# One 512-column matmul over both parts of the activations, with the halves added at eviction

## The chip, the core and the metric

One core of a Trainium2 chip runs the whole program as one launch. The metric is device time in microseconds. The kernel before takes 2003.37 us (median of 3 runs, 2002.3 to 2007.34). All times below are of one profiled execution of it, unless a run is named.

## The reference, cut to what matters

The input is 256 tokens of width 1024. A first block (gated linear attention, spatial gating, and product-key retrieval of experts) is followed by a second block (feed-forward, bidirectional retention with a Fourier branch, feed-forward). Nearly all the arithmetic is products of a 1024-wide activation with a weight. Four of them matter here:

```python
h = jnp.einsum('tkd,td->tk', u, xx)           # experts: scores with all 16384 rows of peer_u
a = (jax.nn.gelu(h) * gg)
u = h @ w_in                                  # second block: q, k, v, g, f, ga, gf
(jax.nn.sigmoid(ga) * r + jax.nn.sigmoid(gf) * fo) @ w_out
(jax.nn.silu(a) * b) @ w2                     # feed-forward, a and b from h @ w13
```

`einsum` over chosen experts is computed as a dense product with all 128 blocks of 128 experts, weighted by a matrix G that is zero where an expert was not chosen.

## The kernel before, in words

Activations stand transposed: 128 partitions, 8 chunks of the width (KD), 256 tokens (T). A unit of weights is a tile of 128 x 1024 float32, 512 KB, loaded by the SP queue into `raw` (three buffers). To keep accuracy with the float32r matmul, each weight is split into a rounded part `whi` and a rest `wlo`: ScalarE casts `raw` to `whi` (L108), VectorE subtracts to get `wlo` (L109). Both have three buffers, so the split of unit n+3 may begin when the matmuls of unit n are over. The activations are split likewise into `hi` and `lo` (`nhi`/`nlo`, `nxh`/`nxl`).

A product is three matmuls for each chunk (`mm3`, L245 to L247): `whi` with `hi`, `whi` with `lo`, `wlo` with `hi`; 24 of them make a unit. They accumulate in one half of a PSUM bank of 512 columns. `fm` (L392) is a unit whose result a function evicts.

`Emit.run` writes the instructions of all engines in program order, and each engine runs its own list in that order. After the matmuls of unit n it issues the split of unit n+3 (`fetch`), and then (`settle`) what was put off with `em.later`: the eviction of unit n. So on ScalarE and on VectorE the split of unit n+3 stands ahead of the eviction of unit n.

The stages that the change touches:

- Expert scores (`expert_u`, L1252): 128 units; ScalarE evicts with Gelu into `act` (two buffers, L1256), and POOL stores it to `uD`. In blocks 64 to 122 the matrix G is built in between: `gbuild` makes 32 sets of four float16 operations on VectorE (L1231 to L1234), and two groups of eight float16 matmuls for each set (L1243, L1244), evicted by ScalarE (L1248). A set is issued two units ahead of the first of its groups.
- Gates `sga` and `sgf` (`ev_gate`, L1667): 16 units, evicted with Tanh. In the same stretch VectorE and ScalarE normalize the context (`ctx`, `y`, L326 to L333) and make decay tables (`dk`, `dw`, `D`).
- Gate of retention (`gunit`, L1754): 16 units, evicted with Silu.
- Second feed-forward (`ffn`, `ctx is None`): its columns 8 to 21, two units each.

Names in the profile: `acc` and `wk` are PSUM banks, `scr` is scratch.

Of the kernel before, what the change touches and what calls it, by code (L numbers as in the profile page):

```python
# [11 lines left out]
F32 = mybir.dt.float32  # L12
F32R = mybir.dt.float32r
F16 = mybir.dt.float16
U16 = mybir.dt.uint16
AF = mybir.ActivationFunctionType
ALU = mybir.AluOpType
# [3 lines left out]
P = 128  # L21
T = 256
D = 1024
KD = D // P
# [10 lines left out]
TKE, GB0, GB1 = 63, 64, 58  # L35
# [102 lines left out]
class Halves:  # L138
# [5 lines left out]
    def __getitem__(self, key):  # L144
        p, d, t = key
        if isinstance(d, slice):
            n = d.start // 4
            return self.t[n][p, d.start - 4 * n:d.stop - 4 * n, t]
        return self.t[d // 4][p, d % 4, t]


def merge(main, fill, first=0, every=1.0):
# [46 lines left out]
def body(ctx, tc, I, out):  # L199
    nc = tc.nc  # L200
    act, dve, pe, pool = nc.scalar, nc.vector, nc.tensor, nc.gpsimd
# [8 lines left out]
    em = Emit(nc, rawp, splp, RAW, 3)  # L210
# [154 lines left out]
    def npair(pl, tag, width=T):  # L365

        full = T + 2 if pl is npool else T
        hi = pl.tile([P, KD, full], F32R, name=tag + "hi", tag=tag + "hi")
        lo = pl.tile([P, KD, full], F32R, name=tag + "lo", tag=tag + "lo")
        return hi[:, :, :width], lo[:, :, :width]  # L370

    def apair():
        return [npool.tile([P, T], F32R, name=n, tag=n, bufs=2) for n in ("ah", "al")]
# [10 lines left out]
    def chunks(o, hi, lo, x, width, order=range(KD)):  # L384

        xh, xl = x
        for k in order:
            sl = slice(k * P, k * P + P)
            mm3(o, hi[:, sl], lo[:, sl], xh[:, k, :width], xl[:, k, :width], k == order[0], k == order[-1])


    def fm(ap, x, evac, bank=bankB):  # L392

        def fn(hi, lo):
            ps = bank()
            chunks(ps[:, :T], hi, lo, x(), T)
            em.later(lambda: evac(ps))
        return ("w", ap, fn)
# [60 lines left out]
    def ffn(w13, w2, y, nx, wk, done, rest, early, ctx=None, mc=None):  # L459

        acc = Acc()
        hold = {}
        items = []

        def gate_c(j):
            ps = hold.pop(("c", j))
            s = wk().tile([P, T], F32, name="cs", tag="cs", bufs=1)  # L470
            act.activation(out=s, in_=ps[:, 0:T], func=AF.Silu)
            dve.tensor_tensor(out=s, in0=s, in1=ps[:, T:], op=ALU.mult)
            em.later(lambda: split(s, *mc(j)))

        def gate(j):
            pa_, pb_ = hold.pop(("ps", j, 0)), hold.pop(("ps", j, 1))
            both = ctx is not None and j >= early
            if j < early:
                s, silu, prod = gate_y(pa_, pb_, wk())
            else:  # L480
                w = 2 * T if both else T
                f = wk().tile([P, w], F32, name="s2", tag="s2", bufs=2)
                s = f[:, :T]

                def silu():
                    act.activation(out=f, in_=pa_[:, :w], func=AF.Silu)

                def prod():
                    dve.tensor_tensor(out=f, in0=f, in1=pb_[:, :w], op=ALU.mult)

            def low():
                hold["m", j] = apair()
                split(s, *hold["m", j])
                if both:
                    split(f[:, T:], *mc(j))

            if j < 2:
                silu()
                if ctx is not None:
                    prod()  # L500
                else:
                    em.later(prod, 1)
                em.later(low, 0 if ctx is not None else 1)
                return

            hold["low", j] = low
            if ctx is not None or j == NFF - 1:
                silu()
                prod()
            else:  # L510
                em.later(silu)
                em.later(prod, 1)

        def bank(j, half):
            if ctx is None:
                return bankA() if j == 2 else bankB()
            return bankA() if j == half == 1 else bankB()

        def up0(sp):
            if ctx is not None:  # L520
                c = hold["c", 0] = bankB()
                for n, (hi, lo) in enumerate(sp):
                    chunks(c[:, n * T:n * T + T], hi, lo, ctx(), T)
            ps = [bank(0, n) for n in range(2)]
            hold["ps", 0, 0], hold["ps", 0, 1] = ps
            mm3s([p[:, :T + 2] for p in ps], sp, *y(), T + 2)
            if ctx is not None:
                em.later(lambda: gate_c(0))

        def up(j, half):  # L530
            def fn(hi, lo):
                ps = hold["ps", j, half] = bank(j, half)
                if j >= early:
                    w = T if ctx is None else 2 * T
                    chunks(ps[:, :w], hi, lo, nx(), w)
                else:
                    if ctx is not None:
                        if half == 1:
                            hold["c", j] = bankA()
                        chunks(hold["c", j][:, half * T:half * T + T], hi, lo, ctx(), T)  # L540
                    chunks(ps[:, :T + 2], hi, lo, y(), T + 2)
                if half == 0:
                    if j < early and ctx is not None:
                        em.later(lambda: gate_c(j))
                    em.later(lambda: gate(j))
            return fn

        def down(j):
            def fn(hi, lo):
                mh, ml = hold.pop(("m", j))  # L550
                acc.step(hi, lo, mh, ml, j == 0, j == NFF - 1)
                f = hold.pop(("low", j + 2), None)
                if f is not None and ctx is None and j + 2 == NFF - 1:
                    em.soon.append(f)
                elif f is not None:
                    em.later(f, 0 if ctx is not None else 1)
                if j == NFF - 1:
                    done(acc)
            return fn

        def begun():
            rest()
            em.later(lambda: gate(0), 0 if ctx is not None else 1)

        items += [("w", [w13[0], w13[NFF]], up0), ("e", None, begun)]
        for j in range(1, NFF):
            items.append(("w", w13[NFF + j], up(j, 1)))
            items.append(("w", w13[j], up(j, 0)))
            if ctx is not None and j > 1:
                items.append(("w", w2[j - 2], down(j - 2)))  # L570
            elif 2 < j < NFF - 1:
                for n in (0, 1) if j == 3 else (j - 2,):
                    items.append(("w", w2[n], down(n)))

        for n in range(NFF - 2 if ctx is not None else NFF - 3, NFF):
            items.append(("w", w2[n], down(n)))
        return items
# [109 lines left out]
    sga = pa.tile([P, KD, T], F32, name="sga")  # L687
# [327 lines left out]
    items = []  # L1015
# [236 lines left out]
    def expert_u(b):  # L1252

        def ev(ps):
            u = B["pu"].tile([P, T], F32, name="act", tag="act", bufs=2)
            act.activation(out=u, in_=ps[:, :T], func=AF.Gelu_apprx_tanh)  # L1256
            pool.dma_start(out=uD[:, b, :], in_=u)  # L1257

        return fm(I["pu"][b], X2, ev)


    def first_q(ns):
# [32 lines left out]
    for j in range(NQ, 16):  # L1295
        n = min(j - 1, sc + (3 if j > NQ else 0))
# [98 lines left out]
    E_ = {}  # L1395
# [132 lines left out]
    def rest_f2():  # L1528
        def f():
            E_["r"] = root(ones_sum(E_["q"][:1], bankA))  # L1530
            table(AF.Silu)
            dve.reciprocal(out=E_["r"], in_=E_["r"])

        def norm():
            E_["nx"] = [E_["fp"].tile([P, KD, T], F32R, name=n) for n in ("nxh", "nxl")]
            late_norm(E_["x"], E_["r"], E_["g"], NX, lambda d: E_["h1"][:, d, :],
                      range(KD), modx[:, 48:56])
        em.later(f)
        em.later(norm, 5)
# [127 lines left out]
    def ev_gate(name, j):  # L1667

        def f(ps):
            act.activation(out=M[name][:, j, :], in_=ps[:, :T], func=AF.Tanh, scale=0.5)  # L1670
        return f


# [79 lines left out]

    def gunit(h, j):  # L1754
        def ev(ps):
            act.activation(out=E_["h1"][:, 4 * (h % 2) + j, :], in_=ps[:, :T], func=AF.Silu)
            if j == 3:
                table(AF.Sqrt)
        return fm(I["wg"][4 * h + j], XN, ev)

    def att_s(h):
        def f():
# [208 lines left out]
    i = [n for n, it in enumerate(f1) if it[0] == "w"][-NFF - 2]  # L1971
    f1[i:i] = [("e", None, lambda: x_gain("norm_mix_2", 24, 16, 0.5))]
    items += f1 + [("e", None, open_k)]
    items += [fm(I["wga"][j], XN, ev_gate("sga", j), bankA if j < 4 else bankB) for j in range(8)]
    items += [fm(I["wgf"][j], XN, ev_gate("sgf", j), bankB if j < 6 else bankA) for j in range(8)]
    items.append(("e", None, open_f))
    for g in range(2):
        items += tm(I["wf"][4 * g:4 * g + 4], [XN], ev_f(g), bankB if g else bankA)
# [121 lines left out]
```

## Time and profile before

| | us |
|---|---|
| median of 3 runs | 2003.37 |
| the profiled execution | 2002.91 |
| its span | 2001.2 |
| TensorE (PE) busy | 1986.2 |
| VectorE (DVE) busy | 1397.1 |
| ScalarE (ACT) busy | 1017.0 |
| POOL busy | 153.3 |

The span goes from the first to the last instruction. A busy PE overlaps its matmuls, so the time of one is read from start to start and not from its duration. The granted clock is at full speed in all 40 slices of the page.

### The profile page before, as it was taken

The page shows a single profiled execution, that of the slowest core. Times are in us where ns is not written, and L with a number is a line of the kernel's source. Part 1 is how long each engine was busy: PE and PEld are TensorE (multiplying, and loading weights), DVE is VectorE, ACT ScalarE, POOL GpSimd, SP SyncE. Part 2 cuts the span into 40 slices and gives each one's busy share as a digit, 9 for nine tenths or more (in the row PEclk, how much of TensorE's full clock was granted, in tenths as well). Part 3 has the DMA queues.
Part 4 walks back from the last instruction along what each step waited for, and adds up shares of the span by engine and source line. Part 5 has one row for each costly group of instructions (what it writes and reads, how often), then busy time and mean ns, then how long its engine had stood idle before and what let it go on. Part 6 is the DMA issues. An engine that isn't in the chain of part 4 may idle for free.

```text
span 2001.2 us, 37792 instructions
## 1 busy us (share of the span) xinstructions
PE 1986.2 (99%) x15348; PEld 1906.4 (95%) x15348; DVE 1397.1 (70%) x2282; ACT 1017.0 (51%) x1510; POOL 153.3 (8%) x296
## 2 busy tenths in 40 slices
PE   9999999999999999999999999999999999999998
PEld 8899999999999999999998888899989999999998
DVE  7668788977776666798876776588654556478555
ACT  6555545456766444545563333245644445446444
POOL 0000011111112101111000000010000000000000
PEclk9999999999999999999999999999999999999999
DMA  7656576766667777887664666677633334455653
GB/s 241 195 160 200 169 225 217 242 211 198 195 192 236 234 235 248 286 291 254 208 220 150 197 193 216 200 242 261 189 125 96 107 107 132 144 176 173 190 184 122
DMA packets 110094, 393.18 MB, mean 196 GB/s; under 512 B 14103, under 2 KB 14487, under 8 KB 109536
## 3 DMA queue, kind: packets, MB, share of 16 engines
q1 hardware_dynamic: 85968, 310.55, 48.5%
q0 software_dynamic: 22944, 77.52, 11.7%
q8 instruction: 120, 1.97, 0.4%
q10 hardware_dynamic: 1008, 2.70, 0.4%
q14 instruction: 54, 0.44, 0.1%
HBM read 371.84 MB, written 18.87 MB: 195 GB/s over the span
## 4 chain that ended last, share of the span: by engine, by line
PE 97%; DVE 1%; DMA 1%; ACT 1%; issue 0%; DVEq 0%; ACTq 0%; POOLq 0%
PE wk L245 18%; PE wk L247 18%; PE wk L246 18%; PE acc L246 10%; PE acc L247 10%; PE acc L245 10%; PE acc L416 2%; PE acc L417 2%; PE acc L418 2%; PE acc L1243 1%; PE acc L1244 1%; DMA raw<-w_dram 0%; PE acc L1080 0%; PE wk L259 0%; DVE wlo L109 0%; PE wk L1898 0%
## 5 line engine op out<-in xcount | busy, mean ns | idle before, releaser
L109 DVE TENSOR_TENSOR wlo<-raw,whi 128x1024 fp32r<-128x1024 f32 x587 | 717.0, 1223 | 494.8 <-ACT whi L108 490.5
L108 ACT CAST whi<-raw 128x1024 fp32r<-128x1024 f32 x587 | 614.8, 1048 | 682.0 <-PE wk L246 323.7
L245 PE MATMUL wk<-nhi,whi 128*128 128x256 f32 (+1 forms) x1744 | 496.9, 285 | 0.0
L247 PE MATMUL wk<-nhi,wlo 128*128 128x256 f32 (+1 forms) x1744 | 491.5, 282 | 0.3 <-DVE wlo L109 0.3
L246 PE MATMUL wk<-nlo,whi 128*128 128x256 f32 (+1 forms) x1744 | 489.7, 281 | 0.0
L246 PE MATMUL acc<-al,whi 128*128 128x256 f32 x1376 | 387.8, 282 | 0.1
L247 PE MATMUL acc<-ah,wlo 128*128 128x256 f32 x1376 | 387.7, 282 | 0.0
L245 PE MATMUL acc<-ah,whi 128*128 128x256 f32 x1376 | 387.7, 282 | 0.0
L246 PEld LDWEIGHTS wk<-nlo,whi 128*128 128x128 f32 x1744 | 329.6, 189 | 0.6 <-issue 0.5
L247 PEld LDWEIGHTS wk<-nhi,wlo 128*128 128x128 f32 x1744 | 329.4, 189 | 0.5 <-DVE wlo L109 0.5
L245 PEld LDWEIGHTS wk<-nhi,whi 128*128 128x128 f32 x1744 | 328.6, 188 | 0.9 <-issue 0.5
L246 PEld LDWEIGHTS acc<-al,whi 128*128 128x128 f32 x1376 | 259.2, 188 | 1.3 <-DVE al L377 0.5
L245 PEld LDWEIGHTS acc<-ah,whi 128*128 128x128 f32 x1376 | 259.2, 188 | 0.9
L247 PEld LDWEIGHTS acc<-ah,wlo 128*128 128x128 f32 x1376 | 259.3, 188 | 0.0
L246 PE MATMUL wk<-nxl,whi 128*128 128x512 f32 (+1 forms) x544 | 188.5, 346 | 0.0
L245 PE MATMUL wk<-nxh,whi 128*128 128x512 f32 (+1 forms) x544 | 188.2, 346 | 0.0
L247 PE MATMUL wk<-nxh,wlo 128*128 128x512 f32 (+1 forms) x544 | 187.4, 344 | 0.0
L376 ACT CAST ah<-early 128x256 fp32r<-128x256 f32 x128 | 52.1, 407 | 170.0 <-PE acc L247 165.2
L247 PEld LDWEIGHTS wk<-nxh,wlo 128*128 128x128 f32 x544 | 102.2, 188 | 13.2
L245 PEld LDWEIGHTS wk<-nxh,whi 128*128 128x128 f32 x544 | 102.1, 188 | 13.0
L246 PEld LDWEIGHTS wk<-nxl,whi 128*128 128x128 f32 x544 | 102.1, 188 | 11.8
L1257 POOL DMA_DIRECT2D uD<-act x128 | 69.3, 542 | 382.1 <-ACT act L1256 319.8
(534 smaller groups left out, 3210.9 us busy)
## 6 DMA issues: line engine op xcount, KB each, us to landing
raw<-pu_dram SPq DMA_DIRECT2D x128, 512.0 KB, 3.8
raw<-pv_dram SPq DMA_DIRECT2D x128, 512.0 KB, 4.3
row<-ada_dram POOLq DMA_DIRECT2D x59, 512.0 KB, 4.5
raw<-f13a_dram SPq DMA_DIRECT2D x44, 512.0 KB, 3.5
raw<-f2a_dram SPq DMA_DIRECT2D x44, 512.0 KB, 4.5
raw<-f13b_dram SPq DMA_DIRECT2D x44, 512.0 KB, 3.5
raw<-w_dram SPq DMA_DIRECT2D x41, 512.0 KB, 4.0
uD<-act POOLq DMA_DIRECT2D x128, 128.0 KB, 3.9
```

The costliest lines, as they stand in the source:

```text
L108: nc.scalar.copy(hi, r)
L109: nc.vector.tensor_tensor(out=lo, in0=r, in1=hi, op=ALU.subtract)
L245: pe.matmul(o, whi, xhi, start=start, stop=False)
L246: pe.matmul(o, whi, xlo, start=False, stop=False)
L247: pe.matmul(o, wlo, xhi, start=False, stop=stop)
L376: act.copy(hi, src)
L416: pe.matmul(o, xh[:, k, ts], hi[:, sl], start=k == 0, stop=False)
L417: pe.matmul(o, xh[:, k, ts], lo[:, sl], start=False, stop=False)
L418: pe.matmul(o, xl[:, k, ts], hi[:, sl], start=False, stop=k == KD - 1)
L1243: pe.matmul(o, p2[:, k, :, t], ph[:, k, :, t], start=True, stop=False)
L1244: pe.matmul(o, p2[:, k, :, t], p1[:, k, :, t], start=False, stop=True)
L1257: pool.dma_start(out=uD[:, b, :], in_=u)
```

## The change

For 125 units (expert blocks 63 to 127, the 16 gates, the 16 retention gates, and 28 of the second feed-forward) `hi` and `lo` of the activations stand side by side in one tile. `whi` meets both in one matmul of 512 columns, and `wlo` meets `hi` in one of 256: 16 matmuls for a unit and not 24. The bank then holds two halves. `fold` adds them: ScalarE copies the second half out of PSUM, VectorE adds the first half to it, and only then ScalarE applies Gelu, Tanh or Silu. Where no 512-column form is used, the two views `hi` and `lo` are read as before.

```diff
+    def wide(ps, hi, lo, x):
+        for k in range(KD):
+            sl = slice(k * P, k * P + P)
+            first = lambda: pe.matmul(ps.rearrange("p (a t) -> p a t", a=2), hi[:, sl], x.both[:, k], start=k == 0,
+                                      stop=k == KD - 1)
+            if k < KD - 1:
+                first()
+            pe.matmul(ps[:, :T], lo[:, sl], x[0][:, k, :], start=False, stop=False)
+            if k == KD - 1:
+                first()
+    def fold(out, ps):
+        act.copy(out, ps[:, T:])
+        dve.tensor_tensor(out=out, in0=ps[:, :T], in1=out, op=ALU.add)
...
-        return hi[:, :, :width], lo[:, :, :width]
+        return Pair(pl.tile([P, KD, 2, full], F32R, name=tag, tag=tag)[:, :, :, :width])
...
-                    act.activation(out=f, in_=pa_[:, :w], func=AF.Silu)
+                        act.activation(out=f, in_=f, func=AF.Silu)
...
+                        u = E_["p"].tile([P, T], F32, name="nn", tag="nn", bufs=3)
+                        fold(u, pb_)
+                        dve.tensor_tensor(out=f, in0=f, in1=u, op=ALU.mult)
+                if not both:
+                    fold(f, pa_)
...
-            act.activation(out=u, in_=ps[:, :T], func=AF.Gelu_apprx_tanh)
+            if b < TKE:
+                act.activation(out=u, in_=ps[:, :T], func=AF.Gelu_apprx_tanh)
+            else:
+                fold(u, ps)
+                act.activation(out=u, in_=u, func=AF.Gelu_apprx_tanh)
...
-            act.activation(out=M[name][:, j, :], in_=ps[:, :T], func=AF.Tanh, scale=0.5)
+            o = M[name][:, j, :]
+            fold(o, ps)
+            act.activation(out=o, in_=o, func=AF.Tanh, scale=0.5)
...
-            act.activation(out=E_["h1"][:, 4 * (h % 2) + j, :], in_=ps[:, :T], func=AF.Silu)
+            o = E_["h1"][:, 4 * (h % 2) + j, :]
+            fold(o, ps)
+            act.activation(out=o, in_=o, func=AF.Silu)
```

ScalarE's list in the expert stage while G is built, two units of the program before; what stands in brackets names the engines or queues whose semaphore is waited for (PE, DVE, DMAHW and DMASW for transfers).

```order
L108 CAST whi<-raw 128x1024 [waits DMAHW3_49,DVE_49,PE_49]
L1248 ACTIVATE G<-acc 128x4x128
L1256 ACTIVATE act<-wk 128x256 [waits DMASW6_49,PE_49,Activation_49]
L108 CAST whi<-raw 128x1024 [waits DMAHW4_49,DVE_49,PE_49]
L1248 ACTIVATE G<-acc 128x4x128
L1256 ACTIVATE act<-wk 128x256 [waits DMASW7_49,PE_49,Activation_49]
```

The same place of the changed program:

```order
L108 CAST whi<-raw 128x1024 [waits DMAHW3_49,PE_49]
L1293 ACTIVATE G<-acc 128x4x128
L412 COPY act<-wk 128x256 [waits DMASW6_49,Activation_49]
L1305 ACTIVATE act<-act 128x256 [waits DVE_49]
L108 CAST whi<-raw 128x1024 [waits DMAHW4_49,PE_49]
L1293 ACTIVATE G<-acc 128x4x128
L412 COPY act<-wk 128x256 [waits DMASW7_49,Activation_49]
L1305 ACTIVATE act<-act 128x256 [waits DVE_49]
```

One instruction for each unit is new on ScalarE, and the Gelu now waits for VectorE, with the next `whi` behind it.

VectorE's list at that place before (`p`, `ph` are the four operations of a set):

```order
L109 TENSOR_TENSOR wlo<-raw,whi 128x1024 [waits DMAHW1_49,PE_49,Activation_49]
L1231 TENSOR_TENSOR p_5511<-iota,i1T 128x1024 [waits PE_49]
L1232 TENSOR_TENSOR p_5512<-iota,i2T 128x1024
L1233 TENSOR_TENSOR ph<-p_5511,ghT 128x1024 [waits DVE_49]
L1234 TENSOR_TENSOR p_5511<-p_5511,glT 128x1024 [waits DVE_49]
L109 TENSOR_TENSOR wlo<-raw,whi 128x1024 [waits DMAHW2_49,PE_49,Activation_49]
L109 TENSOR_TENSOR wlo<-raw,whi 128x1024 [waits DMAHW3_49,PE_49,Activation_49]
```

And now:

```order
L109 TENSOR_TENSOR wlo<-raw,whi 128x1024 [waits DMAHW1_49,Activation_49]
L413 TENSOR_TENSOR act<-wk,act 128x256 [waits DMASW4_49,PE_49,Activation_49]
L1276 TENSOR_TENSOR p_5497<-iota,i1T 128x1024 [waits PE_49]
L1277 TENSOR_TENSOR p_5498<-iota,i2T 128x1024
L1278 TENSOR_TENSOR ph<-p_5497,ghT 128x1024 [waits DVE_49]
L1279 TENSOR_TENSOR p_5497<-p_5497,glT 128x1024 [waits DVE_49]
L109 TENSOR_TENSOR wlo<-raw,whi 128x1024 [waits DMAHW2_49,Activation_49]
L413 TENSOR_TENSOR act<-wk,act 128x256 [waits DMASW5_49,PE_49,Activation_49]
L109 TENSOR_TENSOR wlo<-raw,whi 128x1024 [waits DMAHW3_49,Activation_49]
L413 TENSOR_TENSOR act<-wk,act 128x256 [waits DMASW6_49,PE_49,Activation_49]
```

The addition of a unit stands behind a `wlo`, and in about every second unit that `wlo` stands behind a set.

VectorE's list in the gate stage now, where the context is normalized (before, the same without the L413 rows):

```order
L109 TENSOR_TENSOR wlo<-raw,whi 128x1024 [waits DMAHW6_49,Activation_49]
L335 SCALAR_TENSOR_TENSOR ctx<-ctx,gc,rr 128x256
L342 SCALAR_TENSOR_TENSOR y<-ctx,modc,y 128x256 [waits DVE_49,Activation_49]
L413 TENSOR_TENSOR sga<-wk,sga 128x256 [waits PE_49,Activation_49]
L109 TENSOR_TENSOR wlo<-raw,whi 128x1024 [waits DMAHW7_49,Activation_49]
```

Here the addition stands behind the `wlo` and the two operations on `ctx`; the Tanh waits for it.

## Rows read from the trace of the kernel before

**Rows 1.** The page's head and its busy table: busy us, share of span, instructions.
```profile
span 2001.2 us, 37792 instructions
PE 1986.2 (99%) x15348; PEld 1906.4 (95%) x15348; DVE 1397.1 (70%) x2282; ACT 1017.0 (51%) x1510; POOL 153.3 (8%) x296
```

**Rows 2.** Timeline of PE, units of 256 columns: start, duration, both in us.
```profile
408.06 0.28 PE L245 MATMUL wk<-nhi,whi 128*128 128x256 f32 x1
...
422.68 0.28 PE L245 MATMUL wk<-nhi,whi 128*128 128x256 f32 x1
```

**Rows 3.** Timeline of PE, a unit of 512 columns in the first feed-forward.
```profile
1102.25 0.39 PE L245 MATMUL wk<-nxh,whi 128*128 128x512 f32 x1
...
1106.37 0.39 PE L245 MATMUL wk<-nxh,whi 128*128 128x512 f32 x1
```

**Rows 4.** Timeline of ACT in the expert stage while G is built.
```profile
480.06 1.05 ACT L108 CAST whi<-raw 128x1024 fp32r<-128x1024 f32 x1 [1.06 <-PE wk L246]
481.02 1.13 ACT L1248 ACTIVATE G<-acc 128x512 f32<-128x512 f32 x1
481.92 0.44 ACT L1256 ACTIVATE act<-wk 128x256 f32<-128x256 f32 x1
```

**Rows 5.** Timeline of DVE and PE in the same stretch.
```profile
481.14 1.23 DVE L109 TENSOR_TENSOR wlo<-raw,whi 128x1024 fp32r<-128x1024 f32 x1 [1.51 <-ACT whi L108]
...
482.29 0.68 DVE L1231 TENSOR_TENSOR p<-iota,i1T 128x1024 f16<-128x1024 f16 x1
...
484.21 0.69 DVE L1234 TENSOR_TENSOR p<-p,glT 128x1024 f16<-128x1024 f16 x1
...
484.98 1.23 DVE L109 TENSOR_TENSOR wlo<-raw,whi 128x1024 fp32r<-128x1024 f32 x1
...
487.17 0.23 PE L1243 MATMUL acc<-ph,p 128*128 128x128 f16 x1
```

**Rows 6.** Groups of 420 to 640 us: count, busy us, mean ns, idle before.
```profile
L108 ACT CAST whi<-raw 128x1024 fp32r<-128x1024 f32 x66 | 69.2, 1049 | 70.9 <-PE wk L246 70.3
L109 DVE TENSOR_TENSOR wlo<-raw,whi 128x1024 fp32r<-128x1024 f32 x66 | 80.6, 1222 | 57.4 <-ACT whi L108 57.2
```

**Rows 7.** Timeline of DVE and ACT in the second feed-forward.
```profile
1886.42 0.41 DVE L489 TENSOR_TENSOR s<-s,wk 128x256 f32<-128x256 f32 x1
1886.87 0.41 ACT L376 CAST ah<-s 128x256 fp32r<-128x256 f32 x1 [1.62 <-DVE s L489]
1887.18 1.04 ACT L108 CAST whi<-raw 128x1024 fp32r<-128x1024 f32 x1
```

**Rows 8.** Group over the whole span: a copy of 256 columns out of PSUM.
```profile
L1071 ACT COPY qc<-wk 128x256 f32<-128x256 f32 x6 | 2.2, 367 | 0.0
```

**Rows 9.** Timeline of DVE in the gate stage.
```profile
1394.10 2.02 DVE L265 TENSOR_TENSOR scr<-scr 128x512 f32<-128x512 f32 x3
...
1397.16 0.35 DVE L1680 TENSOR_SCALAR dk<-dw 128x384 f32<-128x384 f32 x1
...
1401.58 1.75 DVE L1061 RECIPROCAL rr<-rr 128x256 f32<-128x256 f32 x1 [0.56 <-ACT rr L349]
...
1407.50 0.48 DVE L326 SCALAR_TENSOR_TENSOR ctx<-ctx,gc,rr 128x256 f32<-128x256 f32 x1
1407.90 0.48 DVE L333 SCALAR_TENSOR_TENSOR y<-ctx,modc,y 128x256 fp32r<-128x256 f32 x1
...
1436.03 0.95 DVE L1703 TENSOR_TENSOR D<-D,dk 128x768 f32<-128x768 f32 x1
```

**Rows 10.** Timeline of ACT in the gate stage.
```profile
1403.23 1.04 ACT L108 CAST whi<-raw 128x1024 fp32r<-128x1024 f32 x1
...
1405.28 1.05 ACT L108 CAST whi<-raw 128x1024 fp32r<-128x1024 f32 x1 [0.72 <-PE wk L246]
```

**Rows 11.** Timeline of ACT, the end of the expert stage.
```profile
646.15 0.39 ACT L1256 ACTIVATE act<-wk 128x256 f32<-128x256 f32 x1 [3.37 <-DMA uD<-act]
```

**Rows 12.** The page's DMA issues: count, KB each, median us to landing.
```profile
uD<-act POOLq DMA_DIRECT2D x128, 128.0 KB, 3.9
```

More of the change, by code (lines that the diff above doesn't have):

```diff
@@ L149, in __getitem__, with __new__ @@
         return self.t[d // 4][p, d % 4, t]
+class Pair(tuple):
+    def __new__(cls, both):
+        self = super().__new__(cls, (both[:, :, 0, :], both[:, :, 1, :]))
+        self.both = both
+        return self
 def merge(main, fill, first=0, every=1.0):
@@ L367, in npair @@
         full = T + 2 if pl is npool else T
-        hi = pl.tile([P, KD, full], F32R, name=tag + "hi", tag=tag + "hi")
-        lo = pl.tile([P, KD, full], F32R, name=tag + "lo", tag=tag + "lo")
-        return hi[:, :, :width], lo[:, :, :width]
+        return Pair(pl.tile([P, KD, 2, full], F32R, name=tag, tag=tag)[:, :, :, :width])
     def apair():
@@ L389, in chunks, with fw, fn @@
             mm3(o, hi[:, sl], lo[:, sl], xh[:, k, :width], xl[:, k, :width], k == order[0], k == order[-1])
+    def wide(ps, hi, lo, x):
[11 more added lines that the diff above has]
+        dve.tensor_tensor(out=out, in0=ps[:, :T], in1=out, op=ALU.add)
+    def fw(ap, x, evac, bank=bankB):
+        def fn(hi, lo):
+            ps = bank()
+            wide(ps, hi, lo, x())
+            em.later(lambda: evac(ps))
+        return ("w", ap, fn)
     def fm(ap, x, evac, bank=bankB):
@@ L485, in silu @@
                 def silu():
-                    act.activation(out=f, in_=pa_[:, :w], func=AF.Silu)
+                    if both:
+                        act.activation(out=f, in_=pa_, func=AF.Silu)
+                    else:
+                        act.activation(out=f, in_=f, func=AF.Silu)
                 def prod():
-                    dve.tensor_tensor(out=f, in0=f, in1=pb_[:, :w], op=ALU.mult)
+                    if both:
+                        dve.tensor_tensor(out=f, in0=f, in1=pb_, op=ALU.mult)
+                    else:
+                        u = E_["p"].tile([P, T], F32, name="nn", tag="nn", bufs=3)
[3 more added lines that the diff above has]
+                    fold(f, pa_)
             def low():
@@ L533, in fn @@
                 if j >= early:
-                    w = T if ctx is None else 2 * T
-                    chunks(ps[:, :w], hi, lo, nx(), w)
+                    if ctx is None:
+                        wide(ps, hi, lo, nx())
+                    else:
+                        chunks(ps, hi, lo, nx(), 2 * T)
                 else:
@@ L1255, in ev @@
             u = B["pu"].tile([P, T], F32, name="act", tag="act", bufs=2)
-            act.activation(out=u, in_=ps[:, :T], func=AF.Gelu_apprx_tanh)
+            if b < TKE:
+                act.activation(out=u, in_=ps[:, :T], func=AF.Gelu_apprx_tanh)
+            else:
+                fold(u, ps)
+                act.activation(out=u, in_=u, func=AF.Gelu_apprx_tanh)
             pool.dma_start(out=uD[:, b, :], in_=u)
-        return fm(I["pu"][b], X2, ev)
+        return (fm if b < TKE else fw)(I["pu"][b], X2, ev)
     def first_q(ns):
@@ L1534, in norm @@
         def norm():
-            E_["nx"] = [E_["fp"].tile([P, KD, T], F32R, name=n) for n in ("nxh", "nxl")]
+            E_["nx"] = Pair(E_["fp"].tile([P, KD, 2, T], F32R, name="nx"))
             late_norm(E_["x"], E_["r"], E_["g"], NX, lambda d: E_["h1"][:, d, :],
@@ L1755, in ev @@
         def ev(ps):
-            act.activation(out=E_["h1"][:, 4 * (h % 2) + j, :], in_=ps[:, :T], func=AF.Silu)
+            o = E_["h1"][:, 4 * (h % 2) + j, :]
+            fold(o, ps)
+            act.activation(out=o, in_=o, func=AF.Silu)
             if j == 3:
                 table(AF.Sqrt)
-        return fm(I["wg"][4 * h + j], XN, ev)
+        return fw(I["wg"][4 * h + j], XN, ev)
     def att_s(h):
@@ L1973, in body @@
     items += f1 + [("e", None, open_k)]
-    items += [fm(I["wga"][j], XN, ev_gate("sga", j), bankA if j < 4 else bankB) for j in range(8)]
-    items += [fm(I["wgf"][j], XN, ev_gate("sgf", j), bankB if j < 6 else bankA) for j in range(8)]
+    items += [fw(I["wga"][j], XN, ev_gate("sga", j), bankA if j < 4 else bankB) for j in range(8)]
+    items += [fw(I["wgf"][j], XN, ev_gate("sgf", j), bankB if j < 6 else bankA) for j in range(8)]
     items.append(("e", None, open_f))
```

## The prediction

> **What bounds the kernel now.** I read the busy table first: PE is busy for 1986.2 of 2001.2 us, and no other engine for more than 70% of the span [rows 1]. So every change to the matmuls counts, and the others count only where they make PE wait. Next comes PE's timeline, from start to start since matmuls overlap: in units of 256 columns 123 matmuls take 422.68 - 408.06 = 14.62 us, 118.9 ns each [rows 2]; in a unit of 512 columns 18 take 4.12 us, 228.9 ns each [rows 3]. A unit before is 24 x 118.9 = 2.85 us. Then the timelines of ACT and DVE in the expert stage: ACT waits 1.06 us for PE before it casts the next weight [rows 4], DVE waits 1.51 us for that cast [rows 5]. Neither is full there: in 220 us ACT's casts wait 70.9 us, DVE's subtractions 57.4 us [rows 6]. Last, the gate stage [rows 9, 10] and the end of the expert stage [rows 11].
>
> **What is removed.** For each chunk three starts of 118.9 ns = 356.7 become 228.9 + 118.9 = 347.8 ns: 8.9 ns saved, 0.07 us for a unit, 8.9 us for 125 units. So the doubled matmul is hardly cheaper than two single ones. No row shows a 512-column matmul that reads two runs, or one between two of 256 columns. Reading the same columns, I give it no gain over 228.9, and at the other end two singles, 237.8, with which the saving is nil. I take 228.9, the row of the same size.
>
> The Trainium skill, "TensorE: Matmul & The Clock Gate", section on the back-to-back issue gap, puts an isolated stream at N/2.4 + 2.5 ns, 109 and 216 ns; the trace has 118.9 and 228.9 here. By the page's figures, as an estimate, a chunk would save 109 + 109 - 216 = 2.5 ns and 125 units 2.5 us, less than a third of what the rows give.
>
> **What is added.** A copy of 256 columns on ACT, 0.37 us [rows 8], and an addition on DVE. DVE's operation on the same shape from PSUM takes 0.41 us, and ACT starts 0.04 us after its end [rows 7]. By sums there is room: ACT per unit would have 0.96 (cast) + 0.90 (G) + 0.37 + 0.44 (Gelu) = 2.7 us [rows 4, 8], against the 3.4 us of a unit with its share of G (worked out below). But the order matters. The Gelu waits for the addition, that stands behind the `wlo` of unit n+3, and that waits for the `whi` which ACT has just made; the next `whi` stands behind the Gelu on ACT's list. So one loop goes through both engines for each unit, and can't overlap with the next. The rows show such a wait already: ACT waited 1.62 us for a DVE operation behind a `wlo`, and the next `whi` started only 0.31 us after the waiting cast did [rows 7].
>
> *Expert stage.* The loop without a set, from addition to addition: handover 0.04, Gelu to `whi` 0.31 [rows 7], cast 0.96, G 0.90 (starts 480.06, 481.02, 481.92) [rows 4], copy 0.37 [rows 8], handover 0.04, addition 0.41 [rows 7]: 3.03 us. The other way round, cast to `wlo` 1.08 and `wlo` 1.15 [rows 4, 5] is done before the copy. With a set DVE alone is the limit: addition 0.33 (0.41 less the 0.08 by which successive operations overlap), set 2.69 (482.29 to 484.98), `wlo` 1.15 (481.14 to 482.29) [rows 5]: 4.17 us. There are 32 sets in 59 units: 32 x 4.17 + 27 x 3.03 = 215.2 us. Five units have a second group of G, 0.90 us each on ACT; half of these fall into loops that are waiting for ACT: 2.2 us, in all 217.4. Before, the stretch of 66 units takes 220 us [rows 6], less seven units without G, 7 x 2.85, is 200.0 us, 3.4 for each of the 59. So DVE and ACT need 17.4 us more than PE took. What lies ahead of that is the lead of a set: the one that ends at 484.90 serves a group that starts at 487.17 [rows 5], 2.3 us. The stretch grows by 17.4 - 2.3 = 15.1 us, as gaps of PE, mostly ahead of the float16 matmuls of G; PE's own saving there, 59 x 0.07 = 4.1 us, is worth nothing, since it only lengthens the gaps.
>
> At the end of the stage ACT waits 3.37 us for a store to free an `act` buffer [rows 11]; in the trace the lead of the weights hides it, and that lead will be used up. Between nothing and 3.37 us; I take 2.5. Expert stage: +17.6 us.
>
> *Gates.* The same loop, longer by the context's operations. Starting at L265 at 1394.10 [rows 9], DVE has 2.02 for that, then three times addition, handover, Tanh to `whi`, cast to `wlo`, `wlo` (0.41 + 0.04 + 0.31 + 1.08 + 1.15 = 2.99, 8.97 together), four operations on `dk` and `dw` of 0.35 that overlap to 1.1, a reciprocal of 1.75, and 0.76 to the next cast: 14.6 us, so the cast that stood at 1403.23 [rows 10] starts at 1408.7 and its `wlo` is done 2.3 us later, at 1411.0. Its unit began at 1408.1 (the cast at 1405.28 was freed by PE [rows 10], it serves the unit two later, and this one is a unit before that): 2.9 us of waiting, the lead is gone. From there a loop with `ctx` and `y` takes 2.99 + 0.40 + 0.40 = 3.79 us (starts 1407.50 and 1407.90 [rows 9]) against 2.85: 0.94 lost, seven times, 6.6 us; two loops with one of the two, 0.5 each; two plain ones 0.14 each; the last one behind a product of 0.95 [rows 9], 1.1. Sum 2.9 + 6.6 + 1.0 + 0.3 + 1.1 = 11.9 us. If the lead were larger than I read, 2.9 less.
>
> *The rest.* The retention gates come in fours after much longer units; the plain loop loses 0.14 us four times, which the lead of two units covers. In the second feed-forward one Silu and two additions fall to three units (8.4 us), and the loops take 3.7 us at most. So PE keeps its saving there and in six expert units: 50 x 0.07 = 3.5 us. If that cover failed, the 16 retention gates would cost 16 x 0.14 = 2.2 us.
>
> **Sum.** 17.6 + 11.9 - 3.5 = +26.0 us. On the profiled execution, 2002.91, that is 2028.9 (its span plus the same 1.7 us around it); the median of the runs, 2003.37, lies 0.46 us above it, so I forecast 2029.4, rounded to 2029. The bounds of the single terms: matmul with two runs, 0 to 3.5 us less gain; lead of a set, 0 to the 5.7 us of two whole units, +2.3 or -3.4; end of stage -2.5 to +0.9; gates -2.9; handovers, if 0.1 us and not 0.04, +5.
>
> **The rivals.** (A) PE gets its saving and the waits stay hidden: 2003.4 - 8.9 = 1994.5. For it speaks that busy sums leave a fifth of each engine free and that weights are split three units ahead; against it that a loop which is longer than a unit uses up any lead, 2.3 us after some eight units (two loops take 7.2 us, two units of PE then 6.64). It would need two loops under 6.64 us. (B) Slower only in the expert stage, where DVE's sum alone makes it; the gates keep their lead, because the context's operations slip behind: 2003.4 + 17.6 - 3.5 - 1.1 = 2016. (C) The store becomes the limit too: `act` has two buffers, the copy claims one, and it is held through copy, addition and Gelu, about 2.4 us in a loop with a set, and the landing, 3.9 us in the median [rows 12], plus the issue. That is 6.4 of the 7.2 us that two loops take. With landings a microsecond longer than that margin, 0.5 us for each pair, 29 times: 2029 + 15 = 2044. (D) No difference: the loops cost just what the saving brings. No row speaks for that balance.
>
> **How the numbers follow.** Forecast 0.60, B 0.17, C 0.12, A 0.06, D 0.05. About 0.3%, 6 us, is what a measurement of this kernel can tell from no change. A is faster by 8.9 us, D the same, the others are slower: 0.06, 0.05, 0.89. With all its bounds on one side the forecast reaches from 2020 (2029 - 3.4 - 2.5 - 2.9) to 2041 (2029 + 2.3 + 0.9 + 5 + 3.5); with B and most of C the range is 2011 to 2045.
>
> **What would show it.** In the changed profile DVE's `wlo` should hardly wait for `whi` where a set stands before it; ACT's Gelu should show waits of one to three microseconds for DVE's addition, 65 times; PE should show gaps of about 0.6 us at the first float16 matmul of a set, one for each two units, and in the gate stage gaps of 0.9 us ahead of a `wlo`. Starts of the new matmuls should be 228.9 and 118.9 ns apart. I am wrong if PE stays without gaps between 440 and 640 us, or if the Gelus wait but `wlo` is still ready in time; then the lead was larger than the rows let me see.

## The result, and the profile after

The changed kernel takes 2032.85 us (median of 4 runs, 2031.61 to 2033.57) against 2002.84 us in the runs beside it: ratio 1.0147, 95% interval 1.0135 to 1.0159, or 30.0 us slower. The forecast was 2029 us, 26 us slower.

The head and the busy table of the changed kernel's page (busy us, share of the span, instructions):

```profile
span 2031.9 us, 36183 instructions
PE 1995.0 (98%) x14348; PEld 1855.4 (91%) x14348; DVE 1441.7 (71%) x2407; ACT 1053.3 (52%) x1635; POOL 153.6 (8%) x296
```

Beside [rows 1]: 1000 matmuls fewer, eight for each of 125 units, and yet a span 30.7 us longer. DVE and ACT have 45 and 36 us more work, with much idle time left on both. So neither is full, and the answer lies in the waits. ACT's waits in the expert stage (420 to 660 us; total, times, longest, in us):

```profile
ACT act L1305 <- DVE act L413: 58.8, 62, 3.7
ACT act L412 <- DMA uD<-act: 5.3, 2, 3.2
```

L1305 is the Gelu, L413 the addition, L412 the copy. In [rows 4] ACT waited here for PE. Now it waits for DVE, once in each unit. ACT's timeline of two units (start, duration, idle before in brackets), where [rows 4] showed one:

```profile
479.75 0.42 ACT L1305 ACTIVATE act<-act 128x256 f32<-128x256 f32 x1 [1.44 <-DVE act L413]
480.07 1.04 ACT L108 CAST whi<-raw 128x1024 fp32r<-128x1024 f32 x1
481.01 1.10 ACT L1293 ACTIVATE G<-acc 128x512 f32<-128x512 f32 x1
481.89 0.43 ACT L412 COPY act<-wk 128x256 f32<-128x256 f32 x1
483.75 0.42 ACT L1305 ACTIVATE act<-act 128x256 f32<-128x256 f32 x1 [1.42 <-DVE act L413]
484.07 1.03 ACT L108 CAST whi<-raw 128x1024 fp32r<-128x1024 f32 x1
485.01 1.11 ACT L1293 ACTIVATE G<-acc 128x512 f32<-128x512 f32 x1
485.91 0.42 ACT L412 COPY act<-wk 128x256 f32<-128x256 f32 x1
486.82 0.42 ACT L1305 ACTIVATE act<-act 128x256 f32<-128x256 f32 x1 [0.49 <-DVE act L413]
487.15 1.03 ACT L108 CAST whi<-raw 128x1024 fp32r<-128x1024 f32 x1
```

DVE at the same place; [rows 5] shows it before (L1276 is the first of the set's four operations):

```profile
479.64 0.68 DVE L1276 TENSOR_TENSOR p<-iota,i1T 128x1024 f16<-128x1024 f16 x1
...
482.16 1.22 DVE L109 TENSOR_TENSOR wlo<-raw,whi 128x1024 fp32r<-128x1024 f32 x1
483.30 0.42 DVE L413 TENSOR_TENSOR act<-wk,act 128x256 f32<-128x256 f32 x1
485.14 1.23 DVE L109 TENSOR_TENSOR wlo<-raw,whi 128x1024 fp32r<-128x1024 f32 x1 [1.42 <-ACT whi L108]
486.36 0.43 DVE L413 TENSOR_TENSOR act<-wk,act 128x256 f32<-128x256 f32 x1
486.70 0.68 DVE L1276 TENSOR_TENSOR p<-iota,i1T 128x1024 f16<-128x1024 f16 x1
```

Each wait can be followed by hand. The Gelu at 483.75 starts when the addition of 483.30 is done. That stands behind the `wlo` of 482.16, and that behind a set. The `whi` at 484.07 stands behind the Gelu, and the `wlo` at 485.14 waits 1.42 us for it. From `whi` to `whi` it is 4.00 us with a set between and 3.08 us without, 7.08 us for two units. PE's two units need less: 16 chunks at 0.353 us (the median start to start there) are 5.6 us, and two groups of G at 0.44 us (485.55 to 485.99 on PE) make it 6.5.

What PE waits for in this stage (420 to 660 us) is the last operation of a set, inside the first group of float16 matmuls; in the kernel before it shows no wait there:

```profile
PE acc L1289 <- DVE p L1279: 6.6, 26, 0.5
```

By PE's start times the first groups of the 32 sets take 25.8 us in all, before 14.1; the second groups take 14.2 and 14.3. These 11.7 us cover the whole loss of the stretch of G in the table below, 11.3.

In the gate stage (waits of 1380 to 1480 us for ACT, 1390 to 1480 us for PE) the same picture, the Tanh in place of the Gelu. In these rows PE waits for a `wlo`, which it never did there before:

```profile
ACT sgf L1721 <- DVE sgf L413: 11.9, 8, 2.8
ACT sga L1721 <- DVE sga L413: 11.4, 8, 2.6
...
PE wk L406 <- DVE wlo L109: 5.3, 8, 0.8
```

Where the time went is read from PE's start times in the two traces:

| place on PE | before | after | later by | step |
|---|---|---|---|---|
| first matmul of G | 432.48 | 432.10 | -0.38 | |
| last matmul of G | 632.95 | 643.84 | +10.89 | +11.27 |
| first 512-column matmul of the first feed-forward | 1039.79 | 1055.41 | +15.62 | +4.73 |
| first matmul of `wf`, behind the 16 gates | 1433.73 | 1459.68 | +25.95 | +10.33 |
| first product with weighted scores (retention) | 1515.14 | 1543.69 | +28.54 | +2.59 |
| last of these | 1701.58 | 1731.85 | +30.28 | +1.74 |
| last matmul | 1992.18 | 2022.61 | +30.43 | +0.15 |

### The profile page after: what moved, and what is told of

The parts are those of the page before. It is cut to its first block, busy times and chain, and to the rows that moved or that the text cites. A ratio compares the mean times of both kernels' runs of the same rounds, so it can differ in the third digit from the quotient of the medians.

```text
span 2031.9 us, 36183 instructions
## 1 busy us (share of the span) xinstructions
PE 1995.0 (98%) x14348; PEld 1855.4 (91%) x14348; DVE 1441.7 (71%) x2407; ACT 1053.3 (52%) x1635; POOL 153.6 (8%) x296
## 3 DMA queue, kind: packets, MB, share of 16 engines
q0 software_dynamic: 22944, 77.52, 11.3%
## 4 chain that ended last, share of the span: by engine, by line
PE 80%; issue 7%; ACT 4%; DVE 4%; DMA 3%; POOL 1%; SPq 0%; DVEq 0%; ACTq 0%; POOLq 0%
PE wk L255 12%; PE wk L254 12%; PE wk L256 12%; PE acc L255 10%; PE acc L256 10%; PE acc L254 10%; PE wk L402 4%; PE wk L406 2%; ACT whi L108 2%; PE acc L449 2%; PE acc L448 2%; PE acc L450 2%; DVE wlo L109 1%; ACT G L1293 1%; DMA uD<-act 1%
## 5 line engine op out<-in xcount | busy, mean ns | idle before, releaser
L254 PE MATMUL wk<-n,whi 128*128 128x256 f32 (+1 forms) x1016 | 288.0, 283 | 0.0
L255 PE MATMUL wk<-n,whi 128*128 128x256 f32 (+1 forms) x1016 | 287.9, 283 | 0.0
L256 PE MATMUL wk<-n,wlo 128*128 128x256 f32 (+1 forms) x1016 | 285.1, 281 | 1.0 <-DVE wlo L109 1.0
L402 PE MATMUL wk<-n,whi 128*128 128x512 f32 x728 | 265.9, 402 | 1.3 <-ACT whi L108 1.3
L406 PE MATMUL wk<-n,wlo 128*128 128x256 f32 x728 | 190.3, 282 | 5.3 <-DVE wlo L109 5.3
L254 PEld LDWEIGHTS wk<-n,whi 128*128 128x128 f32 x1016 | 193.0, 190 | 0.9 <-issue 0.5
L256 PEld LDWEIGHTS wk<-n,wlo 128*128 128x128 f32 x1016 | 191.9, 189 | 1.4 <-DVE wlo L109 1.4
L255 PEld LDWEIGHTS wk<-n,whi 128*128 128x128 f32 x1016 | 191.3, 188 | 0.5 <-issue 0.5
L402 PEld LDWEIGHTS wk<-n,whi 128*128 128x128 f32 x728 | 136.1, 188 | 25.3 <-ACT whi L108 1.6
L406 PEld LDWEIGHTS wk<-n,wlo 128*128 128x128 f32 x728 | 137.4, 189 | 13.6 <-DVE wlo L109 8.6
L255 PE MATMUL wk<-nxl,whi 128*128 128x512 f32 x320 | 125.9, 394 | 0.0
L254 PE MATMUL wk<-nxh,whi 128*128 128x512 f32 x320 | 125.5, 392 | 0.0
L256 PE MATMUL wk<-nxh,wlo 128*128 128x512 f32 x320 | 124.8, 390 | 0.0
```

The source lines that it names most:

```text
L254: pe.matmul(o, whi, xhi, start=start, stop=False)
L255: pe.matmul(o, whi, xlo, start=False, stop=False)
L256: pe.matmul(o, wlo, xhi, start=False, stop=stop)
L402: first = lambda: pe.matmul(ps.rearrange("p (a t) -> p a t", a=2), hi[:, sl], x.both[:, k], start=k == 0, stop=k == KD - 1)
L406: pe.matmul(ps[:, :T], lo[:, sl], x[0][:, k, :], start=False, stop=False)
```

## The experiments

The theory, T1: on each engine instructions run in the order of its list, and the new eviction ties ScalarE and VectorE into one chain for each unit (`whi`, `wlo`, addition, Gelu, next `whi`) that is longer than PE's unit, so PE starves, though both engines have time to spare. Rivals: R1, the 512-column matmul over two runs is itself slow; R2, the added copies and additions are too much work; C, the store out of the two `act` buffers sets the pace. All changes are against the changed kernel unless another is named.

**The activation one unit later.** All instructions stay; only their order on ScalarE changes (a third `act` buffer, with two small constants sharing a tile to make room).

```diff
                 fold(u, ps)
-                act.activation(out=u, in_=u, func=AF.Gelu_apprx_tanh)
+
+                def gelu():
+                    act.activation(out=u, in_=u, func=AF.Gelu_apprx_tanh)
+                    pool.dma_start(out=uD[:, b, :], in_=u)
+                em.later(gelu)
+                return
             pool.dma_start(out=uD[:, b, :], in_=u)
```

(and likewise for Tanh and Silu).

> Same matmuls, same copies, additions and activations as the changed kernel, but ScalarE issues the Gelu, Tanh or Silu of a unit one unit later, behind the next whi, so that it no longer stands waiting for an addition that VectorE has queued behind a wlo (a third act buffer keeps the store out of it). T1, the loop ScalarE-VectorE-ScalarE is what starves TensorE: the wait of act L1305 (58.8 us in 62 times) and of sga/sgf (23.3 us in 16) is gone, the expert stage falls from 217 back to 200 to 204 us and the gates lose most of their 10.5 us: 2001 to 2010 us. Rival R1, the matmul of 512 columns itself is slower or starts later than two of 256: no change, 2033 us. Rival R2, the work of the copy and the addition (0.4 us on each engine and unit) is itself too much, whatever its order: 2025 us or more.

Measured: 2001.1 us (10 runs), ratio to the kernel before 0.9987, interval 0.9977 to 0.9996. All 30 us are gone and a little more. Two groups of 420 to 660 us in this run (count, busy us, mean ns, idle before and its releasers):

```profile
L108 ACT CAST whi<-raw 128x1024 fp32r<-128x1024 f32 x74 | 77.8, 1051 | 56.7 <-PE wk L402 44.1 <-PE wk L255 7.0 <-DMA raw<-pv_dram 4.8
...
L1307 ACT ACTIVATE act<-act 128x256 f32<-128x256 f32 x65 | 26.8, 413 | 2.4 <-DVE act L413 2.4
```

The Gelu's wait fell from 58.8 to 2.4 us, and the cast waits for PE again, as in [rows 6]. The busy table has the same work as the changed kernel's:

```profile
PE 1984.8 (99%) x14348; PEld 1856.1 (93%) x14348; DVE 1441.9 (72%) x2407; ACT 1052.2 (53%) x1635; POOL 153.2 (8%) x296
```

So R2 falls: the same 65 copies and additions in the stage cost nothing once nothing stands behind their wait. This kernel beats both others, the kernel before by 1.8 us (by the interval 0.8 to 4.6).

**The wide matmuls without the addition.**

```diff
-            fold(o, ps)
-            act.activation(out=o, in_=o, func=AF.Tanh, scale=0.5)
+            act.activation(out=o, in_=ps[:, :T], func=AF.Tanh, scale=0.5)
```

(and likewise in the other three evictions).

> The wide matmuls stay, the copy and the addition are left out (the activation reads the first half of the bank alone, so the second half's product is missing from the output). This shows the matmuls alone. T1: nothing of the +30 is left; the gain is the matmuls' own: about 130 units of 8 chunks at 8.9 ns, as the prediction had it from the rows of before, would be -9 us (1994), at the 3 ns by which the pitches of the changed kernel's trace differ from those of before it is -3 us (2000). Rival R1 (the wide form costs): 2015 to 2033.

Measured: 1999.47 us, ratio 0.9983 (0.9973 to 0.9993), 3.4 us faster, 1.4 to 5.4. R1 falls. The saving by 8.9 ns for each chunk, 8.9 us, lies outside the interval; 3.4 us are 3.4 ns for each of 1000 chunks.

**The addition without the wide matmuls.** `whi` meets `hi` and `lo` in two matmuls of 256 columns, the second into the bank's other half.

```diff
-            pe.matmul(ps.rearrange("p (a t) -> p a t", a=2), hi[:, sl], x.both[:, k], ...)
+            pe.matmul(ps[:, :T], hi[:, sl], x[0][:, k, :], ...)
+            pe.matmul(ps[:, T:], hi[:, sl], x[1][:, k, :], ...)
```

> The other half of the change alone: 24 matmuls of 256 columns as before, but the product with the activations' second part goes to the second half of the bank, and the copy and the addition bring it back. T1 (the loop of the eviction is the loss): the whole loss without the matmuls' gain of 3.4 us that the wide matmuls alone showed, 2033 + 3.4 = 2036 us. Rival R1 (the matmul of 512 columns is part of the loss): below 2030 us.

Measured: 2032.94 us, ratio 1.0151 (1.0134 to 1.0168). The whole loss comes with 24 matmuls for a unit as well. The 3.4 us that wide matmuls gain where PE is the bound don't show beside it: 2032.94 against 2032.85. Where PE waits, faster matmuls only lengthen the wait.

**The parts alone.** In each, the other units go back to `fm` and their old eviction.

> The change in the expert stage alone (62 units); gates, gate units of retention and the second FFN as before. If the stages' losses add up: +15.6 us as the start times of the two traces show, 2018.5 us; the forecast's terms had +17.6. If part of what the later stages lost was inherited from here (transfers or order), more than that: 2020 to 2024.

> The change in the 16 gate units alone, all else as before. By the start times of the two traces the gates gave +10.5 us, and the wf products right behind them +2.6. T1a, what comes behind the gates (+4.6 us up to 1760) is inherited from them, because VectorE and ScalarE leave the stage late: 2003 + 13 to 15 = 2016 to 2018 us. T1b, it belongs to the retention gates' own evictions: 2003 + 10.5 = 2013.5 us or a little less.

> The change in the 16 retention gate units and the second FFN alone. T1a (the later loss is inherited from the gates): only the matmuls' gain is left, about 50 units of 8 chunks at 3 ns = -1.2 us, 2001.6 us. T1b (these evictions have a loop of their own): +2 to +4.6 us, 2005 to 2007.5 us. The forecast had -3.5 us for them, 1999.4 us.

> The change in the 16 retention gate units alone. T1b, their evictions have a loop of their own: the heads' stretch (up to the last weighted scores) gains about 1.7 us, as in the run of these and the second FFN together, and the total is that run's, 2008.9, or 0.2 above it (of it 2.9 us are the slower pv stretch). If the second FFN was what cost there: 2003 to 2006 us.

| part alone | us | ratio to before (95%) |
|---|---|---|
| expert stage | 2015.56 | 1.0059 (1.0042 to 1.0076) |
| gates | 2019.88 | 1.0085 (1.0069 to 1.0102) |
| retention gates and second feed-forward | 2008.89 | 1.0026 (1.0015 to 1.0038) |
| retention gates | 2008.61 | 1.0030 (1.0018 to 1.0041) |

These add to more than the whole (12.7 + 16.4 + 5.5 = 34.6 by the medians). The start times of the last three runs showed why: each loses 2.4 to 2.9 us between 648 and 1040 us, in the `pv` rows (the products behind the expert scores), where nothing of the change stands but the layout of the activations' tiles. So the next run had that alone.

**The layout alone.** The `Pair` stays, all units use `fm` and the old evictions.

> Only the layout of the change: hi and lo parts of the activations lie side by side in one tile (the Pair), all matmuls and evictions as in the kernel before. In the runs with the gates alone and with the second FFN and the retention gates alone, 2.9 us were lost between the first matmul of the pv rows and the first FFN, where nothing of the change stands: matmuls of 256 columns 119.74 ns apart there, 118.67 ns in the kernel before. If the layout does it: 2003 + 3 = 2006 us, with that pitch. If not: 2003 us, and the loss there belongs to the timing of those two kernels.

Measured: 2007.21 us, ratio 1.0018 (1.0009 to 1.0028): +3.8 us by the medians, and +3.7 of them in the `pv` rows. Against that as the base the gates alone cost 2019.88 - 2007.21 = 12.7 us, the retention gates 1.4, with the second feed-forward 1.7. Together with the expert stage's 12.7 that is 27.1 of 30.0 us. (From the first matmul of G to the first feed-forward the expert stage alone loses 14.1 us in its trace, in the changed kernel 16.0. Its run had the fast pace in the `pv` rows, so it is compared with the kernel before.)

Of the two theories on what follows the gates each had a part right. In the run with the gates alone the `wf` products behind them still lost 2.8 us: VectorE leaves the gates late, T1a (PE and its weight loads wait there for `wlo`, 1.1 and 2.5 us at L449, which they don't in the kernel before). In the runs with the retention gates the heads still lost 1.7 us of their own, T1b. In the changed kernel's trace (1455 to 1760 us) PE and its weight loads wait there for `scl`, the low part of the weighted scores, where the kernel before shows no such wait:

```profile
PE wk L255 <- DVE scl L384: 1.1, 4, 0.3
...
PEld wk L255 <- DVE scl L384: 2.1, 4, 0.6
```

**A third `act` buffer.** (`bufs=2` becomes `bufs=3`, nothing else.)

> The changed kernel with three act buffers in place of two, so that the copy of a unit no longer waits for the store of the unit two before (two constants of one column share a tile, to make room). T1: only the two waits of act L412 for a store go (5.3 us of ScalarE at the end of the expert stage, of which the forecast had 2.5 us reach TensorE), 2028 to 2031 us. Rival C, the store sets the pace of the expert stage: the stage loses most of its 15.6 us, 2018 us or less.

Measured: 2029.31 us, ratio 1.0135 (1.0118 to 1.0152), some 3.5 us less than the changed kernel, and the loss from the first matmul of G to the first feed-forward is 11.8 us in place of 16.0. So the store costs what it blocks at the end of the stage, and rival C falls: it doesn't set the pace.

**The whole eviction ahead of the next split.**

```diff
-            em.later(lambda: evac(ps))
+            em.soon.append(lambda: evac(ps))
```

> The changed kernel with the whole eviction of the expert, gate and retention gate units (copy, addition, activation) issued ahead of the next unit's whi and wlo, in place of behind the whi and the wlo. ScalarE still waits for VectorE's addition, but that no longer stands behind a wlo; it still stands behind the four G masks in every second expert unit. T1 (the queue position makes the price, 1.42 us per wait, not that one engine waits for another, 0.5 us): most of the loss goes, 2001 to 2010 us. Rival R3 (any wait of ScalarE for VectorE in each unit costs, because the whi stands behind it): 2020 us or more.

Measured: 2086.32 us, ratio 1.0418 (1.0401 to 1.0436), 83 us slower than before and 53 slower than the changed kernel. Of T1's two versions the expectation had put the wrong one forward: the place behind the `wlo` isn't the price. ACT and DVE over one set (timeline, columns as above):

```profile
502.66 0.42 ACT L1305 ACTIVATE act<-act 128x256 f32<-128x256 f32 x1 [2.92 <-DVE act L413]
502.99 1.03 ACT L108 CAST whi<-raw 128x1024 fp32r<-128x1024 f32 x1
503.93 2.02 ACT L1293 ACTIVATE G<-acc 128x512 f32<-128x512 f32 x2
505.76 0.41 ACT L412 COPY act<-wk 128x256 f32<-128x256 f32 x1
506.65 0.42 ACT L1305 ACTIVATE act<-act 128x256 f32<-128x256 f32 x1 [0.49 <-DVE act L413]
506.98 1.03 ACT L108 CAST whi<-raw 128x1024 fp32r<-128x1024 f32 x1
```

```profile
499.68 0.68 DVE L1276 TENSOR_TENSOR p<-iota,i1T 128x1024 f16<-128x1024 f16 x1
...
502.21 0.42 DVE L413 TENSOR_TENSOR act<-wk,act 128x256 f32<-128x256 f32 x1
504.05 1.23 DVE L109 TENSOR_TENSOR wlo<-raw,whi 128x1024 fp32r<-128x1024 f32 x1 [1.42 <-ACT whi L108]
506.19 0.42 DVE L413 TENSOR_TENSOR act<-wk,act 128x256 f32<-128x256 f32 x1 [0.92 <-ACT act L412]
508.04 1.23 DVE L109 TENSOR_TENSOR wlo<-raw,whi 128x1024 fp32r<-128x1024 f32 x1 [1.42 <-ACT whi L108]
509.18 0.69 DVE L1276 TENSOR_TENSOR p<-iota,i1T 128x1024 f16<-128x1024 f16 x1
```

Set, addition, Gelu, `whi`, G, copy, addition, Gelu, `whi`, `wlo`, next set: almost nothing lies beside anything else, and here a set follows the last after 9.50 us (499.68 to 509.18), with a second group of G in the chain. Most sets, with one group for each unit, follow after 8.60 us, against 7.06 us in the changed kernel (479.64 to 486.70). In the changed order the `whi` and the copy of ScalarE at least run beside VectorE's set and `wlo`. So the price is the length of the chain through both engines, and R3 was the better theory. Deferring the activation opens the chain; moving all of it forward closes it tighter.

**One stall ahead of the `pv` rows**, to learn whether the loss of the layout hangs on timing: in the last set the first mask is written 14 times.

```diff
-            dve.tensor_tensor(out=p1, in0=keys, in1=of(i1T), op=ALU.is_equal)
+            for _ in range(14 if g == 31 else 1):
+                dve.tensor_tensor(out=p1, in0=keys, in1=of(i1T), op=ALU.is_equal)
```

> The layout alone, as before, and the first mask of the last G set written 13 times more by VectorE, 7.9 us, so that TensorE waits once, some 12 us ahead of the pv rows. In the run with the layout alone the pv rows' matmuls were 120.0 ns apart (46.08 us for 384), in all runs in which TensorE had waited in the expert stage 118.67 ns (45.57 us for 384), whatever the layout. If the timing with which TensorE enters the stage sets that pace: it goes to 45.57 us here, and the time is 2007 + 3 to 6 (the stall) - 3.3. If the addresses of the layout set it: it stays 46.08 us, 2010 to 2013 us.

> The kernel before with the same 13 extra masks. Its pace in the pv rows was 45.57 us for 384 matmuls. If only the timing matters, it can fall to 46.08 us here (or stay); if the addresses matter alone, it stays at 45.57 us: 2003 + 3 to 6 us of stall.

Measured: 2016.06 us with the layout, 2011.84 us with the kernel before, 8.9 and 8.5 us above those without a stall. PE waited at one place, in the first of them 6.8 us at a stretch, and the `pv` rows kept their pace: 46.08 us for 384 matmuls with the new layout, 45.57 us with the old. A stall at this place doesn't change it. It lies 20 us ahead of the rows (the wait ends at 636.7 us, the rows start at 656.9), with expert units between. The 14 masks took 10.12 us, 9.4 more than one, and not the 7.9 us that were expected, so little of them was taken up by a lead.

## Why the prediction was right, and where it wasn't

**The mechanism was right.** The Gelu waited for the addition 62 times, 0.95 us in the mean and 3.7 at most. The loop was forecast at 4.17 us with a set and 3.03 without; it measured 4.00 and 3.08. PE's gaps came where the prediction put them, at the float16 matmuls of a set, 0.4 us each in the mean and not 0.6; half of the Gelu's waits were nearer 0.5 us than the one to three it named. The 0.17 us too much in the loop with a set are one term: the set, put at 2.69 us from 482.29 to 484.98 in [rows 5], takes 2.52 in the changed kernel (479.64 to 482.16). One reading was off: the prediction took VectorE alone for the limit where there is a set. The run with the activation deferred has the same set, addition and `wlo` for each unit, and the stretch of G is 198.9 us there, against 200.5 before and 211.7 changed. So it is the chain also there; the number came out because VectorE's part fills the chain at that place. That part was luck.

**Expert stage: +17.6 forecast, +16.0 in the trace.** Of it 11.3 lie in the stretch of G, forecast 15.1: 32 loops of 4.00 and 27 of 3.08 us are 211.2 us, and the stretch took 211.7. Two terms of the forecast hardly show. Of the five second groups of G four fell into loops with a set, which stayed at 4.00 us, and the other loop took 3.94: 0.9 us and not 2.2. And the lead of 2.3 us that was set against the loss isn't there where the loss begins: in both kernels the first group starts just as the first set ends (0.0 us), and only later sets of the kernel before end some 1.8 us ahead of theirs. The other 4.7 lie behind the stretch, forecast 2.5; in the run with the third buffer 1.8 of them are left.

**Gates: +11.9 forecast, +10.3 in the trace**, 12.7 as a part alone with what they leave to the `wf` products. The seven loops with `ctx` and `y` were put at 3.79 us; from `whi` to `whi` they take 3.77.

**The rest: -3.5 forecast, +4.5 in the trace.** This is the step that failed, twice. "So PE keeps its saving there": the second feed-forward and the tail gain nothing that shows (+0.15; the same stretch moved by -1.0 to +0.7 us in runs that leave it as it was). And the prediction thought the lead of two units would cover the retention gates, 2.2 us if it failed; it failed, for 1.4 to 1.7 us, though not at the weights, where the prediction looked, but at the low part of the scores, one more operation in VectorE's list. That the gates' delay would run on into the `wf` products, 2.6 to 2.8 us, no step had.

**The matmuls' saving was 3.4 us, not 8.9.** Each chunk was to save 356.7 - 347.8 ns. In three retention gate units of the changed kernel:

```profile
1524.01 0.40 PE L402 MATMUL wk<-n,whi 128*128 128x512 f32 x1
...
1532.45 0.28 PE L254 MATMUL wk<-qxh,kxh 128*128 128x256 f32 x1
```

24 chunks take 8.44 us, 351.7 ns each. That is 5 ns less than [rows 2] and 4 more than the 228.9 + 118.9 of [rows 3] and [rows 2]: between matmuls of 256 columns, and reading two runs, the one of 512 isn't as close to the next as in a row of its own kind. No run separates these two. In other stages the old chunk was cheaper than [rows 2]: in the second feed-forward the means went from 353.5 to 351.1 ns, 2.3 ns. The Trainium skill, "TensorE: Matmul & The Clock Gate", section on the back-to-back issue gap, gave 2.5 ns for each chunk by its formula for an isolated gap, 2.5 us in all as an estimate. The run without the addition agrees with it (3.4 us, 1.4 to 5.4), and not with the 8.9 taken from the rows; the page's two gaps, 109 and 216 ns, are still not those of this trace.

**The rivals.** A's mechanism is that of the deferred run, which differs by the order of one engine's list, and ends at 2001.1 and not at 1994.5. B lost its condition, since the gates lost 10 us. C was wrong in the size: the store's waits come to 5.3 us of ScalarE. D, no difference, lies outside the interval.

## What to carry to other kernels

When an eviction is split between two engines that also prepare the next operands, follow one unit round both lists: if its chain comes back to the next operand's first step and is longer than the bound engine's unit, its length, not either engine's load, is the pace. Here the same work was free once the last step of the eviction stood one unit later. And a gain on the bound engine counts only in the stages where it doesn't wait: 3.4 us here alone, nothing beside the loop.

## What was not expected of the hardware

The `pv` rows run at one of two paces. One group of PE's matmuls of 750 to 1000 us, in the kernel before and then with the layout alone (count, busy us, mean ns, idle before):

```profile
L247 PE MATMUL acc<-ah,wlo 128*128 128x256 f32 x699 | 196.7, 281 | 0.0
```

```profile
L256 PE MATMUL acc<-ah,wlo 128*128 128x256 f32 x692 | 196.6, 284 | 0.0
```

In the same 250 us seven fewer of this third of the matmuls: 118.67 ns from start to start in the one and 120.0 in the other, with the same instructions, no waits, and the clock granted in full. All runs with wide matmuls in the expert stage had the fast one for most of the rows (the run with the deferred activation and the one without the addition nearly so, 118.9 in the mean), with the same layout. So the layout alone doesn't explain it. Two things more show in the start times. The rows begin slowly in all six runs in which units of 24 matmuls on the new layout stand right before them. And each change of pace lies where two starts are 0.25 us or more apart; between such pauses the pace is constant. With the retention gates alone it goes from slow to fast at 858.5 us, where two starts lie 0.43 us apart; in the run with the additions and without wide matmuls the first 23 steps take 120 ns, and behind waits of 1.1 and 1.0 us the rows are fast. Not each pause changes it. A pace that is taken over from the units ahead and kept until PE pauses would fit, and the two runs with a stall don't test it, since units stood between their stall and the rows. The cause stays open. It is worth 3.7 us here, about what the wide matmuls gain, so a part that is tried alone should be compared with a run that has the same layout and the same pace.
